# Split input weights kept in DRAM for the later token groups of a hybrid layer

## The chip, the cores and the metric

The kernel runs on one core of one Trainium2 chip. The metric is the device time of one execution in microseconds. Times of several executions are given by their median; one further execution was profiled, and all rows below come from it. Engines are called by the names of the profile: PE is TensorE (PEld its weight loads), DVE is VectorE, ACT is ScalarE, POOL is GpSimd, and SP is SyncE, whose queue here issues all DMAs.

## The reference

One layer, computed for two sets of streams that share the weights: one prompt of 2048 tokens without a past, and 8 running streams with 16 new tokens each. `D_MODEL` is 1024, the projection `w_in` has 7308 columns, all data is fp32.

```
def hybrid_layer(x, p, S_rwkv, shift, S_ssm, conv_buf, k_cache, v_cache):
    h = rms_norm(x, p['norm_w'])
    u = h @ p['w_in']
    ua, ga, zb, xbc, dtb, qc, kc, vc, gc = jnp.split(u, IN_SPLITS, axis=-1)
    oa, S_rwkv, shift = rwkv7_branch(ua, ga, S_rwkv, shift, p)
    ob, S_ssm, conv_buf = mamba2_branch(zb, xbc, dtb, S_ssm, conv_buf, p)
    oc, k_new, v_new = stick_breaking_branch(qc, kc, vc, gc, k_cache, v_cache, p)
    y = x + (jnp.concatenate([oa, ob, oc], axis=-1) @ p['w_out']).astype(x.dtype)
    return y, (S_rwkv, shift, S_ssm, conv_buf, k_new, v_new)
```

The RWKV-7 branch is a linear recurrence with a matrix state for each of 12 heads, the Mamba-2 branch a chunked scan with a convolution in front, the stick-breaking branch an attention whose weights come from a product of `1 - sigmoid` from the right. What the change touches is the second line, `h @ w_in`.

## The kernel before

**Groups.** The 2176 tokens are cut into four groups: 512 prompt tokens and all 128 tokens of the running streams in the first, 512 prompt tokens in each of the others. `h` of one group stays in SBUF, transposed, as a high part `hh` and a low part `hl`. The columns of `w_in` pass by once for every group, so each is loaded four times.

**Products in two parts.** PE multiplies in fp32r, which is fp32 rounded to fewer bits. So each factor is split: `whi` is the weight cast to fp32r on ACT, `wlo` is the rest, `raw - whi`, by a subtraction on POOL (helper `wsplit`, line 537). A product is three matmuls that add up in PSUM: `whi hh`, `whi hl` and `wlo hh`. Results go to PSUM tiles called `pd`.

**Weight tiles.** `wtile` (line 529) gives three tiles of 128 x 536: `wraw` from a ring of four, `whi` and `wlo` from rings of five each. Two functions load weights of the input:

- `wload(cols)` (line 542): 128 columns in two halves of 512 rows; a half is one DMA of 256 KB, one cast and one subtraction. It feeds `dense_t`, where the weights are stationary and up to 512 tokens stream. It is called 39 times in a group (RWKV's k, r, v, gate and low-rank columns, the convolution's channels, the attention's gate).
- `wload_n(spec)` (line 552): 256 columns (268 for one of them, which takes 12 columns of `dt` along by a second small DMA) in four quarters of 256 rows. It feeds `dense_n`, where 128 tokens are stationary and the columns stream. It is called 9 times in a group (q, k, v of the attention, the gate z of Mamba-2).

That is 39 x 2 + 9 x 4 = 114 pieces in a group and 456 in the program. The output projection of the first two branches, `project_ab` (line 590), takes tiles from the same rings for pieces of `w_out` and of the branch outputs `oT`; of those some are split on DVE, the others on POOL.

**Other names.** `fs` and `DN` (lines 989 to 999) are the small DVE operations by which RWKV inverts 16 x 16 blocks; they lie between a store of `GB` to the DRAM scratch `dA`, a load as `AT`, a store to `dD` and a load as `Da`. `RV`, `pz`, `py`, `SE`, `ZY` belong to RWKV's chain over chunks, `rq_m`, `rq_y` and `rq_t` to the inverse square roots, `ab` is a load of the scan's sums.

**What sets the order.** Instructions are not issued as the code is read. A planner (`class Plan`) collects a whole part of the program (the first group in two parts, then the other three groups in one, then the attention) and places instruction after instruction on its engine, always the one that can start first by a small cost model; rings of tiles are handed out in program order. The order that it finds is fixed for every engine and for the queue of SP. An instruction that waits holds up those behind it on its engine, and a DMA that waits for its slot holds up the DMAs behind it.

**Attention stage.** From 3048 us on no weights of the input are used any more.

Of the kernel before, what the change touches and what calls it, by code (L numbers as in the profile page):

```python
# [7 lines left out]
F32 = mybir.dt.float32  # L8
F32R = mybir.dt.float32r
# [423 lines left out]
def build(tc, nc, A, O):  # L433
    ctx = ExitStack()
    with ctx:
        _build(ctx, tc, nc, A, O)


def _build(ctx, tc, nc, A, O):
    plan = Plan(tc)  # L440
    V, S, G, T, Y = (plan.engine(e, x) for e, x in zip("VSGTY", (nc.vector, nc.scalar, nc.gpsimd, nc.tensor, nc.sync)))
# [4 lines left out]
    wp = ph.enter_context(tc.tile_pool(name="w", bufs=2))  # L446
# [6 lines left out]
    dr = ctx.enter_context(tc.tile_pool(name="scratch", bufs=1, space=DRAM))  # L453
# [4 lines left out]
    def pg():  # L458
        return pp.tile([128, 512], F32, name="pg", tag="pg", bufs=3)
# [10 lines left out]
    def f32(ap):  # L470
        return ap.bitcast(F32)
# [29 lines left out]
    win = A["w_in"][0]  # L501
# [24 lines left out]
        (eng_lo or V).tensor_tensor(lo, raw, f32(hi), ALU.subtract)  # L526


    def wtile(n):

        return [wp.tile([128, 536], F32 if nm == "wraw" else F32R, name=nm, tag=nm, bufs=4 if nm == "wraw" else 5)[:, 0:n]
                for nm in ("wraw", "whi", "wlo")]

    def tw(n):
        return wp.tile([128, 536], F32, name="tw", tag="tw", bufs=4)[:, 0:n]
# [1 line left out]
    def wsplit(raw, hi, lo, eng):  # L537
        S.copy(hi, raw)
        eng.tensor_tensor(lo, raw, f32(hi), ALU.subtract)
        return hi, lo  # L540

    def wload(cols):

        res = []
        for half in range(2):
            raw, hi, lo = wtile(512)
            Y.dma_start(raw.rearrange("p (k c) -> p k c", c=128),
                        win[512 * half:512 * half + 512, cols:cols + 128].rearrange("(k p) c -> p k c", p=128))
            res.append([x.rearrange("p (k c) -> p k c", c=128) for x in wsplit(raw, hi, lo, G)])
        return res  # L550

    def wload_n(spec):

        n = sum(c for _, c in spec)
        res = []
        for q in range(4):
            raw, hi, lo = wtile(2 * n)
            r3 = raw.rearrange("p (k c) -> p k c", c=n)
            o = 0
            for c0, cn in spec:  # L560
                Y.dma_start(r3[:, :, o:o + cn],
                            win[256 * q:256 * q + 256, c0:c0 + cn].rearrange("(k p) c -> p k c", p=128))
                o += cn
            res.append([x.rearrange("p (k c) -> p k c", c=n) for x in wsplit(raw, hi, lo, G)])
        return n, res

    def dense_t(h, w, c, n):
# [90 lines left out]
    def sb_weights(kind, j):  # L658

        c0 = {"q": C_Q, "k": C_SK, "v": C_SV}[kind]  # L660
        return wload_n([(c0 + 256 * j, 256)] + [(C_DT, 12)] * (kind == "q" and j == 0))
# [63 lines left out]
    def sb_gate(g, h, j):  # L725
        w = wload(C_SG + 128 * j)
        for u in g.pieces:
            p = dense_t(h, w, u.c0, u.n)
            o = tw(u.n)
            silu2(o[:, :u.n], p[:, :u.n], u.n)  # L730
            for c, n, t in g.segs(u.c0, u.n):
                Y.dma_start(gS[j, :, t:t + n], o[:, c - u.c0:c - u.c0 + n])
# [56 lines left out]
    def rwkv_pre(g, h, pool):  # L789
        w = wload(C_LO)  # L790
        ws, as_ = [x[:, 0:512] for x in h[2:4]] or [pool.tile([128, g.n], F32R, name=x, bufs=1) for x in ("ws", "as")]
        for u in g.pieces:
            n = u.n
            c = slice(u.c0, u.c0 + n)
            p = dense_t(h, w, u.c0, n)
            us = tw(n)
            shift(g, pool, p, u, 18, us)
            th = tw(n)[0:64]
            S.activation(th, us[0:64], AF.Tanh)
            V.tensor_copy(ws[0:64, c], th)  # L800
            V.tensor_tensor(ws[64:128, c], th, f32(ws[0:64, c]), ALU.subtract)
            V.tensor_copy(as_[64:128, c], us[64:128])
            V.tensor_tensor(as_[0:64, c], us[64:128], f32(as_[64:128, c]), ALU.subtract)
        return ws, as_

    def rwkv_dense(g, h, pr, pool, nms, D):
        for nm in nms:
            c0 = {"k": C_K, "r": C_R, "v": C_V, "g": C_G}[nm]
            w = wload(c0 + 128 * pr)
            if nm == "v":  # L810
                full = pool.tile([128, g.n + 128], F32, name="usv", tag="usv", bufs=2)
                G.memset(full[:, 0:64], 0.0)
                G.memset(full[:, 64 + g.n:128 + g.n], 0.0)
                D[nm] = full
                o = full[:, 64:64 + g.n]
            else:
                D[nm] = o = pool.tile([128, g.n], F32, name="us" + nm, tag="us" + nm, bufs=2 if nm == "k" else 1)
            for u in g.pieces:
                p = dense_t(h, w, u.c0, u.n)
                oc = o[:, u.c0:u.c0 + u.n]  # L820
                if nm == "g":
                    silu2(oc, p[:, :u.n], u.n)
                else:
                    shift(g, pool, p, u, c0 // 128 + pr, oc)
# [542 lines left out]
    def ssd_parts(g, h, pool, nb):  # L1367
# [25 lines left out]
        def gates(j):  # L1393

            w = wload_n([(C_Z + 256 * j, 256)])
            if j == 1:
                z1 = st["z"] = pool.tile([128, nt, 128], F32, name="zz", tag="zz", bufs=1)
            for ti, (c, p0) in enumerate(g.tiles):
                p = dense_n(h, w, c)
                z = tw(256)  # L1400
                if j == 1:
                    s = tw(256)
                    S.activation(s, p[:, 0:256], AF.Tanh, scale=0.5)
                    V.scalar_tensor_tensor(z[:, 0:128], s[:, 0:128], 1.0, p[:, 0:128], ALU.add, ALU.mult)
                    V.scalar_tensor_tensor(z1[:, ti, :], s[:, 128:256], 1.0, p[:, 128:256], ALU.add, ALU.mult)
                    gate(0, ti, 256, z[:, 0:128])
                else:
                    silu2(z, p[:, 0:256], 256)
                    gate(j // 2, ti, 64 * j, z)
                    if j == 2:  # L1410
                        gate(1, ti, 0, st["z"][:, ti, :])
# [130 lines left out]
    def following(gi, nh):  # L1542

        ng = GROUPS[gi + 1]
        rs = []
        return [lambda: rs.append(h_scale(ng.tiles))], [lambda: nh.extend(stage_h(ng, rs[0]))], pieces(ng, nh, "v0 q0 v1 k0 q1 k1")
# [47 lines left out]
    for i in range(2):  # L1594
        o = 64 * i
# [9 lines left out]
    for i in range(2):  # L1605
        o = 64 * i
# [41 lines left out]
    p = pg()  # L1648
# [54 lines left out]
    p = pg()  # L1703
# [7 lines left out]
    p = pg()  # L1711
# [12 lines left out]
    for d in dD:  # L1724
        m = NCH * 8 * 2064 + 128
        for i in range(0, m, 128 * 323):
            n = min(128 * 323, m - i)
# [14 lines left out]
    with tc.tile_pool(name="r0", bufs=1) as pool:  # L1742
        rw.send((pool, fill))
        w = tw(512).rearrange("p (a c) -> p a c", c=128)
        p = pg()
# [16 lines left out]
    with tc.tile_pool(name="r", bufs=1) as pool:  # L1762
        for gi in range(1, len(GROUPS)):
            g = GROUPS[gi]
            h, nh, fill = nh, [], {}
            gates = [lambda j=j, h=h: sb_gate(g, h, j) for j in range(4)]
            prj = [lambda a=a: project_ab(*a, lambda: wtile(512), pd, lambda: tw(512)) for a in proj_parts(GROUPS[gi - 1])]
            parts = ssd_parts(g, h, pool, 1)

            late, dense = prj[-1:], prj[:-1] + gates  # L1770
            a, b = parts[1:13], parts[13:]
            s = [parts[0]] + a[:5]
            for l in (a, b):
                if l is b:
                    s += b[:5]
                for f in l[5:9]:
                    s += [f] + dense[:1]
                    dense = dense[1:]
                s += l[9:]
            spread(fill, s + dense, 0, 10)  # L1780
            if gi + 1 < len(GROUPS):
                f8, f, x = following(gi, nh)
                fill[7].extend(f8)
                fill.setdefault(10, []).extend(f + late)
                fill.setdefault(11, []).extend(x)
            else:
                fill.setdefault(11, []).extend(late)
            st = stage_rwkv(g, h, pool, 3)
            next(st)
            st.send((pool, fill))  # L1790
        plan.emit()


    with tc.tile_pool(name="fin", bufs=1) as pool:
        r = pool.tile([64, 6, 128], F32, name="r")
        for q in range(2):
            p = pg()
# [7 lines left out]
        for q in range(2):  # L1805
            p = pg()
# [6 lines left out]
        p = pg()  # L1813
# [25 lines left out]
    p = pt()  # L1839
# [240 lines left out]
```

## Time and profile before

| | |
|---|---|
| runs | 3867.2 us median of 3 (3865.2 to 3870.8) |
| the profiled execution | 3871.6 us, its span 3869.9 us |
| instructions | 68238 |
| mean granted clock of PE | 0.933 |
| bytes moved | 454 MB, a mean of 117 GB/s |
| busy time of POOL and ACT on splits of weights and of `oT` (`wlo`, `whi`) | 762.4 us (568 subtractions), 428.7 us (702 casts) |

The span is the time from the first to the last instruction in the profile. A row of a group of instructions reads: line, engine, operation, out<-in by the program's names, shapes, count, then busy us and mean ns of one, then the engine's idle time in front of them and what ended it. All instructions are recorded at the one line where the planner issues them (L420), so groups are told apart by their tiles. A row of one tile reads: count, then shortest, median and longest ns. A row of waits reads: who waited for whom, us in total, times, longest us. The chain of work is followed back from the last instruction, at each step to what released it.

### The profile page before, as it was taken

Reading aid. Unit: us, or ns where it says so; the run is one execution under the profiler, and the core shown is the slowest. Engines: PE = TensorE matmul, PEld = TensorE weight load, DVE = VectorE, ACT = ScalarE, POOL = GpSimd, SP = SyncE. Lnnn points to the kernel's source line nnn. Section 1 sums busy time; section 2 is a strip of 40 time slices with the busy share of each in tenths; the row PEclk is TensorE's granted clock in tenths of the full one; section 3 lists DMA queues with packets and bytes.
Section 4 is the critical chain, followed back from the end, with each engine's and each line's share of the span. In section 5 each row is a group of like instructions: output and inputs, shape, how many; then the busy total and the mean of one; then the engine's idle time right before and its main releaser. Section 6 shows DMA issues by size and latency. Waiting matters only on the chain. (4 is left out here: it accounts for less than half of the span.)

```text
span 3869.9 us, 68238 instructions
## 1 busy us (share of the span) xinstructions
PE 3385.2 (87%) x23086; PEld 2749.6 (71%) x23086; DVE 2746.8 (71%) x6621; ACT 1724.5 (45%) x4134; POOL 1672.4 (43%) x2621
## 2 busy tenths in 40 slices
PE   7988999977988898988889998888999688989998
PEld 7877888867776676776667777766777555666665
DVE  7657778876698778657886875688778553456665
ACT  4544444433454444434444443445444343445554
POOL 4544555434555655644456555445555323000000
PEclk9998999978989899999899999989999889999999
DMA  4332333335425433553254336324532587765542
GB/s 120 97 107 61 95 92 78 78 103 145 121 59 158 140 89 101 153 149 94 71 154 110 78 84 180 101 68 128 150 82 64 154 212 223 176 150 140 135 129 66
DMA packets 693227, 454.41 MB, mean 117 GB/s; under 512 B 259978, under 2 KB 617806, under 8 KB 692878
## 3 DMA queue, kind: packets, MB, share of 16 engines
q1 hardware_dynamic: 692878, 450.06, 43.7%
q8 instruction: 183, 3.00, 0.3%
q14 instruction: 166, 1.36, 0.1%
HBM read 362.40 MB, written 87.51 MB: 116 GB/s over the span
## 5 line engine op out<-in xcount | busy, mean ns | idle before, releaser
L420 POOL TENSOR_TENSOR wlo<-wraw,whi 128x512 fp32r<-128x512 f32 (+1 forms) x568 | 762.4, 1348 | 542.0 <-ACT whi L420 378.9
L420 ACT CAST whi<-wraw 128x512 fp32r<-128x512 f32 (+1 forms) x702 | 428.7, 620 | 407.7 <-PE pd L420 290.7
L420 PE MATMUL pd<-hh,whi 128*128 128x512 f32 (+1 forms) x1560 | 552.8, 390 | 13.6 <-ACT tw L420 10.7
L420 PE MATMUL pd<-hh,wlo 128*128 128x512 f32 (+1 forms) x1560 | 553.2, 389 | 4.4 <-POOL wlo L420 4.4
L420 PE MATMUL pd<-hl,whi 128*128 128x512 f32 (+1 forms) x1560 | 555.9, 390 | 0.0
L420 PEld LDWEIGHTS pd<-hh,whi 128*128 128x128 f32 x1560 | 296.0, 196 | 51.3 <-ACT tw L420 14.3
L420 PEld LDWEIGHTS pd<-hh,wlo 128*128 128x128 f32 x1560 | 296.3, 194 | 39.5 <-POOL wlo L420 6.4
L420 POOL TENSOR_SCALAR SE<-RV,ELl 64x64 f32<-64x64 f32 x384 | 208.1, 542 | 267.7 <-DVE RV L420 218.8
L420 PEld LDWEIGHTS pd<-hl,whi 128*128 128x128 f32 x1560 | 296.8, 195 | 34.4 <-issue 1.5
L420 PE MATMUL pd<-whi,hh 128*128 128x256 f32 (+1 forms) x1224 | 300.1, 299 | 6.2 <-DVE tw L420 3.7
L420 PE MATMUL pd<-wlo,hh 128*128 128x256 f32 (+1 forms) x1224 | 298.4, 298 | 1.3 <-POOL wlo L420 1.3
L420 PE MATMUL pd<-whi,hl 128*128 128x256 f32 (+1 forms) x1224 | 295.5, 295 | 0.2 <-DVE hl L420 0.2
L420 DVE TENSOR_TENSOR_SCAN I<-ke,I,zeros 128x512 f32<-128x512 f32 x192 | 231.8, 1266 | 82.6 <-ACT ke L420 82.6
L420 ACT COPY aT<-pt 128x512 f32<-128x512 f32 (+3 forms) x320 | 162.4, 524 | 201.8 <-PE pt L420 199.2
L420 PEld LDWEIGHTS pd<-whi,hh 128*128 128x128 f32 x1224 | 214.8, 198 | 11.4 <-DVE tw L420 4.1
L420 PE MATMUL pt<-ident,I 128*128 128x128 f32 x1088 | 180.1, 286 | 42.2 <-DVE I L420 35.9
L420 PE MATMUL zt<-kk,qt 128*128 128x512 f32 (+3 forms) x640 | 205.8, 411 | 11.7 <-DMA kk<-kS 5.7
L420 PEld LDWEIGHTS pd<-wlo,hh 128*128 128x128 f32 x1224 | 213.8, 198 | 3.0 <-POOL wlo L420 2.0
L420 PEld LDWEIGHTS pd<-whi,hl 128*128 128x128 f32 x1224 | 213.0, 198 | 1.8 <-DVE hl L420 0.4
L420 POOL TENSOR_TENSOR oc<-oc,gy 128x512 f32<-128x512 f32 x16 | 20.8, 1302 | 438.2 <-ACT aT L420 167.1
L420 DVE TENSOR_TENSOR fs<-AT,DN 32x63 f32<-32x63 f32 (+14 forms) x672 | 199.6, 297 | 12.3 <-POOL DN L420 0.5
L420 PEld LDWEIGHTS pt<-ident,I 128*128 128x128 f32 x1088 | 120.4, 143 | 115.0 <-issue 36.9
(408 smaller groups left out, 8176.7 us busy)
## 6 DMA issues: line engine op xcount, KB each, us to landing
wraw<-in_w_in SPq DMA_DIRECT2D x456, 256.0 KB
wraw<-in_w_out SPq DMA_DIRECT2D x168, 256.0 KB
kk<-kS SPq DMA_DIRECT2D x160, 256.0 KB
wraw<-oT SPq DMA_DIRECT2D x78, 256.0 KB
ab<-acS SPq DMA_DIRECT2D x34, 384.0 KB
Da<-dD SPq DMA_DIRECT2D x96, 128.0 KB
sraw<-in_x_prompt SPq DMA_DIRECT2D x48, 256.0 KB
pr<-in_w_out SPq DMA_DIRECT2D x48, 256.0 KB
```

The source lines that it names most:

```text
L420: r = f(*a, **k).ins
```

## The change

The first group loads and splits a piece as before, and then stores both parts to a DRAM scratch tile of its own, `wS`, one for each set of columns. When another group asks for the same columns, a single DMA brings both parts back, and there is no raw load, no cast and no subtraction. For this `whi` and `wlo` become the two halves of one tile, `whl`, 128 x 2 x 536, from a ring of five; `wraw` keeps its ring of four. Pieces of `w_out` and `oT` in `project_ab` are still split in every group, with tiles of the same rings. A store is 512 KB, and so is a load of both parts.

```diff
+    def whl(n):
+        return wp.tile([128, 2, 536], F32R, name="whl", tag="whl", bufs=5)[:, :, 0:n]
+
+    def wraw(n):
+        return wp.tile([128, 536], F32, name="wraw", tag="wraw", bufs=4)[:, 0:n]
+
     def wtile(n):
-        return [wp.tile([128, 536], F32 if nm == "wraw" else F32R, name=nm, tag=nm, bufs=4 if nm == "wraw" else 5)[:, 0:n]
-                for nm in ("wraw", "whi", "wlo")]
+        x = whl(n)
+        return wraw(n), x[:, 0], x[:, 1]
+
+    wS = {}
+
+    def wparts(key, q, pieces, n, load):
+        x = whl(n)
+        if q not in wS.setdefault(key, []):
+            if not wS[key]:
+                wS[key].append(dr.tile([pieces, 128, 2, n], F32, name=f"wS{len(wS)}"))
+            wS[key].append(q)
+            raw = wraw(n)
+            load(raw)
+            wsplit(raw, x[:, 0], x[:, 1], G)
+            Y.dma_start(wS[key][0][q], f32(x))
+        else:
+            Y.dma_start(f32(x), wS[key][0][q])
+        return x[:, 0], x[:, 1]
...
     def wload(cols):
...
-            raw, hi, lo = wtile(512)
-            Y.dma_start(raw.rearrange("p (k c) -> p k c", c=128),
-                        win[512 * half:512 * half + 512, cols:cols + 128].rearrange("(k p) c -> p k c", p=128))
-            res.append([x.rearrange("p (k c) -> p k c", c=128) for x in wsplit(raw, hi, lo, G)])
+            def load(raw):
+                Y.dma_start(raw.rearrange("p (k c) -> p k c", c=128),
+                            win[512 * half:512 * half + 512, cols:cols + 128].rearrange("(k p) c -> p k c", p=128))
+            res.append([x.rearrange("p (k c) -> p k c", c=128) for x in wparts(cols, half, 2, 512, load)])
```

`wload_n` is changed in the same way, with `tuple(spec)` as the key and four pieces of `2 * n` columns.

More of the change, by code (lines that the diff above doesn't have):

```diff
@@ L556, in wload_n, with load @@
         for q in range(4):
[L557 to L564, printed above, removed]
+            def load(raw):
+                r3 = raw.rearrange("p (k c) -> p k c", c=n)
+                o = 0
+                for c0, cn in spec:
+                    Y.dma_start(r3[:, :, o:o + cn],
+                                win[256 * q:256 * q + 256, c0:c0 + cn].rearrange("(k p) c -> p k c", p=128))
+                    o += cn
+            res.append([x.rearrange("p (k c) -> p k c", c=n) for x in wparts(tuple(spec), q, 4, 2 * n, load)])
         return n, res
```

## The prediction

> **What bounds the kernel now.** I read the page first, then the busy time by stretches, then the chain of work, and last the weight tiles by themselves. The stretches are cut where the work changes: up to 930 us mostly the first group, up to 3048 us mostly groups two to four, behind that the attention stage.
>
> ```profile
> PE 3385.2 (87%) x23086; PEld 2749.6 (71%) x23086; DVE 2746.8 (71%) x6621; ACT 1724.5 (45%) x4134; POOL 1672.4 (43%) x2621
> 0.00:930.00 930.00, 812.73 (x6545) 734.67 (x6546) 683.19 (x2005) 401.53 (x1085) 455.66 (x945) 0.93 0.37 96
> 400.00:600.00 200.00, 185.81 (x1681) 167.86 (x1680) 158.19 (x502) 85.33 (x244) 108.05 (x251) 1.00 0.37 90
> 930.00:3048.00 2118.00, 1860.21 (x11874) 1525.92 (x11872) 1615.93 (x4105) 929.93 (x2236) 1129.59 (x1556) 0.93 0.41 112
> 3048.00:3870.00 822.00, 712.30 (x4669) 488.98 (x4669) 447.70 (x513) 393.05 (x814) 87.18 (x121) 0.94 0.60 156
> 2473.00:3010.00 537.00, 482.19 (x3131) 387.59 (x3132) 438.38 (x1153) 244.77 (x601) 294.20 (x427) 0.94 0.36 94
> ```
>
> Behind a stretch and its length stand the busy us of PE, PEld, DVE, ACT and POOL, then the granted clock, the DMA share and GB/s. In the later groups (930 to 3048) PE is busy 88% of the time and idle for 258 us; DVE is busy 76%, POOL 53%, ACT 44%. PE is the fullest, but the chain of work of the last whole group (2473 to 3010) says that it is not alone:
>
> ```profile
> by line: PE pd L420 23.1%; PE pg L420 9.1%; DVE DN L420 5.3%; DVE fs L420 5.0%; issue 4.7%; POOL wlo L420 4.7%; DVE BK L420 4.1%; DVE ST L420 4.1%; PE pz L420 3.6%; DVE tw L420 3.6%; ACT tw L420 1.9%; PE py L420 1.8%; DVE wlo L420 1.7%; DMA
> ```
>
> The names shown hold 72.7% of that stretch: PE 37.6, DVE 23.8, POOL 4.7, the rest ACT and issue. The path goes back and forth between PE and DVE, so what delays DVE delays the group. What delays DVE is in the timeline, a weight split on POOL beside the small DVE operations of the RWKV inverse:
>
> ```profile
> 1904.61 1.27 POOL L420 TENSOR_TENSOR wlo<-wraw,whi 128x512 fp32r<-128x512 f32 x1 [2.15 <-ACT whi L420]
> 1904.64 1.30 DVE L420 TENSOR_TENSOR fs<-AT,DN 32x55 f32<-32x55 f32 x1
> 1906.72 0.20 DVE L420 TENSOR_TENSOR fs<-AT,DN 32x48 f32<-32x48 f32 x1
> 1908.02 1.67 POOL L420 TENSOR_TENSOR wlo<-wraw,whi 128x512 fp32r<-128x512 f32 x1
> 1908.47 1.27 DVE L420 TENSOR_TENSOR fs<-AT,DN 32x39 f32<-32x39 f32 x1
> L420 DVE TENSOR_TENSOR fs<-AT,DN x504: 151/201/1342, 1027.0 to 2980.1; 32x28 f32<-32x28 f32 x24, 32x55 f32<-32x55 f32 x24, 32x39 f32<-32x39 f32 x24, 32x60 f32<-32x60 f32 x24
> L420 DVE TENSOR_TENSOR DN<-DN,fs x504: 152/200/1368, 1027.3 to 2980.4; 32x28 f32<-32x28 f32 x24, 32x55 f32<-32x55 f32 x24, 32x39 f32<-32x39 f32 x24, 32x60 f32<-32x60 f32 x24
> 930.00:3048.00 2118.00, 298.88 (x1008) 0.93 0.41 112
> ```
>
> The same kind of instruction takes 0.20 us alone and 1.30 us when a POOL `wlo` holds something that both need; both DVE instructions end with the POOL one. The last row, of the tile `fs` alone, is the mean: 298.88/1008 = 297 ns against a median of 200, so about 97 us are lost in these two lines alone. I did the same for every DVE instruction from 930 to 3048: its duration less the 15th percentile of its own kind and shape, counted where that is over 0.1 us and a POOL `wlo` overlaps it most. That gives 276 instructions with 275 us lost; the first and the last of them, each with its POOL partner:
>
> ```profile
> 936.45 1.28 POOL L420 TENSOR_TENSOR wlo<-wraw,whi 128x512 fp32r<-128x512 f32 x1 [1.18 <-ACT whi L420]
> 936.61 1.15 DVE L420 TENSOR_SCALAR rq_m<-sss 128x8 f32<-128x8 f32 x1
> ...
> 3046.63 2.97 POOL L420 TENSOR_TENSOR wlo<-wraw,whi 128x512 fp32r<-128x512 f32 x2 [0.27 <-ACT whi L420]
> 3047.15 1.23 DVE L420 TENSOR_TENSOR rq_t<-rq_y 128x4 f32<-128x4 f32 x1
> ```
>
> **The change part by part.** The weights of the input are 456 pieces, 114 in each of four groups.
>
> ```profile
> L420 POOL TENSOR_TENSOR wlo<-wraw,whi 128x512 fp32r<-128x512 f32 (+1 forms) x568 | 762.4, 1348 | 542.0 <-ACT whi L420 378.9
> L420 ACT CAST whi<-wraw 128x512 fp32r<-128x512 f32 (+1 forms) x702 | 428.7, 620 | 407.7 <-PE pd L420 290.7
> wraw<-in_w_in SPq DMA_DIRECT2D x456, 256.0 KB
> 930.00:3048.00 2118.00, 104.55 (x134) 345.25 (x567) 583.76 (x432) 0.93 0.41 112
> L420 SPq DMA_DIRECT2D wraw<-in_w_in x472: 367/374/1724, 7.8 to 2976.8; - x158
> ```
>
> *Removed: 342 splits.* In groups two to four 342 casts (0.620 us) leave ACT, 212 us, and 342 subtractions (1.348 us) leave POOL, 461 us. Neither engine is full, so as busy time this is worth nothing; it counts through DVE. The fourth row is the tile `wraw` alone: 432 POOL subtractions from 930 on, which cost DVE 275 us, 0.64 us each. So 342 x 0.64 = 217 us of DVE time go. How much of it lies on the path: at least the named DVE rows, 23.8% of 537 = 128 us of 438 busy, a share of 0.29; at most all that is not named otherwise as well (23.8 + 27.3 = 51.1%, 274 us), 0.63. I split the unnamed part as the named one, 23.8/72.7 = 0.33 of the path, 176 us of 438, a share of 0.40. That is -87 us (bounds -63 and -137). What is late next is PE: its best 200 us show it 93% busy, and 1860/0.93 = 2000 would be 118 us less than the 2118, so PE leaves room for 87 but not for 137.
>
> The Trainium skill, "SBUF — State Buffer", section "Who interferes with whom", says of this row that a VectorE instruction with two SBUF inputs and a GpSimd instruction that reads SBUF exclude each other, and that the one that comes second is blocked for the first one's whole length. The trace agrees, 1.30 against 0.20 us. Taken alone the rule would let each subtraction block DVE for all of its 1.35 us, 461 us in all; the measured 0.64 us says that DVE meets about half of it.
>
> *Removed from the path itself: POOL `wlo`.* It has 4.7% of the chain shown; by 342/432 of that over 2118 us this would be -79 us. But the wait for a weight does not vanish, the landing of a DMA takes its place, so I take 0 for both together and keep -79 as an end.
>
> *Changed: 342 loads.* They now bring 512 KB straight into the five slots of the parts, where a 256 KB load went into one of four raw slots ahead of them.
>
> ```profile
> 2657.97 2.57 DMA ab<-acS
> 2670.75 2.54 DMA wraw<-in_w_out
> GB/s 56 0 0 0 0 0 0 0 0 0 0 0 0 256 323 348 364 338 343 353 287 10 0 0 0 0 0 82 0 0 0 0 0 0 0 0 0 0 0 0
> 1909.61 0.39 PE L420 MATMUL pd<-hh,whi 128*128 128x512 f32 x1
> 1909.84 0.39 PE L420 MATMUL pd<-hh,wlo 128*128 128x512 f32 x1
> ACT whi L420 <- PE pd L420: 214.8, 164, 7.1
> PEld pd L420 <- POOL wlo L420: 21.9, 35, 3.0
> PE pd L420 <- POOL wlo L420: 11.0, 19, 2.6
> SPq L420 <- POOL wlo L420: 620.5, 254, 11.7
> ```
>
> From the end of a slot's last matmul to its next use there were a cast and a subtraction, 0.62 + 1.35 = 2.0 us and what their engines were busy with. Now there is an issue of 0.37 us and a landing: 2.5 us for 256 KB, and another 256 KB at about 340 GB/s (the third row, where one load runs alone) is 0.8 us, so 3.7 us, 1.7 us more. The cover is the ring: matmuls of 512 columns start 0.23 us apart, a piece has 12 of them, 2.8 us, and with one piece in use four others lie ahead, 11 us. So I cost it at nothing; today's waits of PE on the split, 21.9 + 11.0 = 33 us, stand for what becomes a wait on the DMA. Without the cover it is 342 x 1.7 = 581 us, the outer bound on the slow side. The bytes: 342 x 256 KB more over 2118 us are 42 GB/s on top of 112, which by the share per GB/s lifts 0.41 to 0.56; the attention stage lives with 0.60.
>
> SP now waits for PE's last read where it waited for POOL 254 times, 620 us in all. Behind such a wait stand `ab`, the round trip of the RWKV inverse through `dA` and `dD`, stores and loads of other tiles. One blocking wait replaces another of about the same number, so 0, bounds -20 to +40 us (a 254th part of 620, 2.4 us, on every third of some 50 such DMAs of the chain, to either side).
>
> *Added: 114 stores of 512 KB in the first group.* SP issues 114 x 0.37 = 42 us more, each behind the subtraction it waits for; 60 MB over 930 us are 64 GB/s, which lifts its share from 0.37 to 0.61. The split stays there, so DVE gains nothing. A slot is held until the store has read it, while PE reads the same slot for 2.8 us after the split, which hides most of it. I take +5 us, bounds 0 and +42.
>
> *Untouched:* the attention stage, 822 us. The planner makes a new order with its own costs; I take +0, give or take 10.
>
> **Sum.** -87 + 0 + 0 + 0 + 5 = -82 us. The profiled execution took 3871.6 us (span 3869.9), so 3789.6; it lies 4.4 us above the median of 3867.2, so the median comes to 3785 us, 2.1% less.
>
> **The rivals.** First, *off the path*: DVE gives its 217 us back as idle time, because the dense matmuls of PE, 23.1% of the chain, close every gap. For it: PE 88% busy. Against it: 258 us of idle PE, and DVE rows with a quarter of the chain. Time 3867.
>
> Second, *both ends pay*: the upper DVE share and the `wlo` of the chain go too. -137 - 79 is more than PE leaves at its present clock, but the clock of 0.93 would rise with fewer gaps (1.00 in the row 400 to 600). PE's room of 118 plus half of the 7% of 2118 us, 74, is -192, with +5: 3680. For it: ACT and POOL get free besides. Against it: PE would have to be as dense all through as in its best stretch.
>
> Third, on the other side, *late weights*: with nine pieces under way before (five split, four raw) and five now, PE waits for landings of the parts, in `PEld pd`, released by a DMA. For it: in 164 casts of 567 the slot had just been freed by PE, so the ring is already short at times, and projection pieces, with six matmuls, use a slot in 1.4 us. Against it: PE waited for the split only 33 us. It turns the result when the 342 loads cost more than 82/342 = 0.24 us each; at half of the 1.7 us, +291 - 82, it is 4076; at 0.4 us, 3922.
>
> Fourth, *the stores hold the ring*: the slots of the first group come free only when a store has landed, 2.5 us by the row above, 290 us if all of it shows; it decides from 0.72 us a store. Then 3785 + 100 = 3885 for a third. Against it is PE's own use of the slot. The Trainium skill, "DMA: Bandwidth & Descriptors", section "Anatomy of one DMA", puts most of a fixed cost of about 2 us down to the receipt of the write and calls HBM the heaviest target. By that figure it would be, as an estimate, 114 x 2.0 = 228 us; no run shown here has a store from this ring.
>
> That the later groups would not find their parts can be left out: the page's 456 pieces are four times 114, the same columns.
>
> **How the numbers follow.** Forecast 0.70 (3730 to 3850), off the path 0.08, both ends pay 0.08, late weights 0.10, stores 0.04. Within 0.2%, 8 us, is about what a measurement of this kernel can tell from no change. Faster: 0.70 + 0.08 and a little of the first rival, 0.80; same 0.07; slower 0.13. The range, with the lower bounds of the unknown costs and up to where the gain is nearly gone: 3700 to 3862; beneath it lies half of the second case, above it the slow ones and most of the first.
>
> **What would show it.** In the later groups POOL loses about 461 us and ACT 212; the mean of `fs` and `DN` falls from 297 towards 225 ns; DVE's busy time from 930 on falls by about 200 us; PE's share there rises from 88 to 91 or 92%. Wrong would be: DVE falls as said and PE's share does not rise (off the path); large waits of `PEld pd` on `DMA whl<-wS` (late weights); a first group that is longer by over 20 us (stores).

## The result and the profile after

The changed kernel takes 3691.6 us (median of 4 runs, 3687.4 to 3698.0) against 3866.2 us before: a ratio of 0.9555, with a 95% interval of 0.9535 to 0.9574. That is 175 us less, where 82 were forecast, and 3691.6 us lies under the range of 3700 to 3862. The head of the changed kernel's page, its bytes, and the shares of its chain by engine:

```profile
span 3688.1 us, 67232 instructions
PE 3306.9 (90%) x23086; PEld 2683.9 (73%) x23086; DVE 2524.9 (68%) x6621; ACT 1530.7 (42%) x3792; POOL 1210.8 (33%) x2279
HBM read 452.20 MB, written 147.37 MB: 163 GB/s over the span
PE 50%; DVE 28%; issue 6%; ACT 6%; DMA 6%; POOL 3%; SPq 1%; DVEq 0%; POOLq 0%; ACTq 0%
```

POOL has lost 461.6 us, the 342 subtractions, and ACT 193.8, where 212 were forecast for the casts. DVE has as many instructions as before (6621) and yet is busy for 222 us less, close to the 217 us forecast. PE has the same 23086 matmuls and is busy for 78 us less. Its mean granted clock was 0.956 against 0.933 before, and busy time times clock is nearly the same (3161 and 3158 us), so the higher clock accounts for the 78 us.

Next the stretches of the changed kernel, cut at the same places of the work: groups two to four end at 2875 us now. The row with one pair of numbers is of the tile `fs` alone (DVE), and the last two are rows of the whole chain between 2310 and 2830 us, and of the tiles `fs` and `DN`.

```profile
930.00:2875.00 1945.00, 1802.66 (x12021) 1481.10 (x12020) 1406.10 (x4128) 754.32 (x1923) 696.87 (x1240) 0.97 0.56 169
2875.00:3688.00 813.00, 702.43 (x4669) 481.65 (x4669) 446.10 (x512) 392.96 (x814) 88.14 (x120) 0.96 0.61 157
930.00:2875.00 1945.00, 226.47 (x1008) 0.97 0.56 169
by line: PE pd L420 38.3%; PE pg L420 9.1%; issue 4.9%; DVE ST L420 3.7%; DVE DN L420 3.1%; DVE BK L420 3.0%; DVE fs L420 2.5%; DMA whl<-wS 2.5%; PE pz L420 2.4%; DVE tw L420 1.9%; PE py L420 1.8%; DVE RV L420 1.7%; DVE whl L420 1.5%; DVE Y
```

PE's share of the later groups went from 88 to 93%, its idle time from 258 to 142 us, its clock from 0.93 to 0.97. `fs` and `DN` fell from 297 to 225 ns a piece (226.47/1008). On the chain PE's dense matmuls, `PE pd`, have 38% of this stretch of the last group, where they had 23% of the prediction's (the two stretches do not begin at quite the same place of the work).

The first copy `ZY<-pz` of each group's RWKV chain is a good marker of the same point of the work. Differences between markers give each part its own time (the last column is taken before rounding):

| from the first `ZY` of a group to that of the next | before | after | difference |
|---|---|---|---|
| head, up to the first group's | 376 | 391 | +14 |
| first group | 641 | 648 | +7 |
| second | 754 | 688 | -66 |
| third | 727 | 645 | -82 |
| fourth (to the last `ZY`) | 542 | 494 | -47 |
| rest, with the attention | 831 | 823 | -9 |

So the head and the first group pay 21 us, and the later ones bring 195.

What PE and SP wait for in the changed kernel, 930 to 2875 us:

```profile
PEld pd L420 <- DMA whl<-wS: 13.2, 18, 2.1
PE pd L420 <- DMA whl<-wS: 13.0, 16, 1.9
SPq L420 <- PE pd L420: 410.4, 192, 9.9
```

The loads of both parts make PE wait for 26 us in all. SP now waits for PE, 192 times, where it waited for POOL 254 times.

### The profile page after: what moved, and what is told of

Same layout as the page of the kernel before. It is cut to its first block, busy times and chain, and to the rows that moved or that the text cites. A ratio compares the mean times of both kernels' runs of the same rounds, so it can differ in the third digit from the quotient of the medians.

```text
span 3688.1 us, 67232 instructions
## 1 busy us (share of the span) xinstructions
PE 3306.9 (90%) x23086; PEld 2683.9 (73%) x23086; DVE 2524.9 (68%) x6621; ACT 1530.7 (42%) x3792; POOL 1210.8 (33%) x2279
## 4 chain that ended last, share of the span: by engine, by line
PE 50%; DVE 28%; issue 6%; ACT 6%; DMA 6%; POOL 3%; SPq 1%; DVEq 0%; POOLq 0%; ACTq 0%
PE pd L420 28%; PE pg L420 7%; DVE I L420 5%; PE ot L420 3%; PE acc L420 3%; PE pz L420 3%; PE pt L420 3%; DVE tw L420 2%; PE py L420 2%; DVE ST L420 2%; DVE DN L420 2%; DMA whl<-wS 2%; DVE rq_t L420 2%; DVE BK L420 2%; PE zt L420 2%
## 5 line engine op out<-in xcount | busy, mean ns | idle before, releaser
L420 PE MATMUL pd<-hh,whl 128*128 128x512 f32 (+1 forms) x3120 | 957.2, 385 | 12.8 <-ACT tw L420 4.3
L420 PEld LDWEIGHTS pd<-hh,whl 128*128 128x128 f32 x3120 | 563.8, 193 | 81.4 <-ACT tw L420 7.1
L420 PE MATMUL pd<-hl,whl 128*128 128x512 f32 (+1 forms) x1560 | 543.9, 384 | 0.0
L420 PE MATMUL pd<-whl,hh 128*128 128x256 f32 (+1 forms) x2448 | 482.4, 294 | 22.7 <-DMA whl<-wS 8.9
L420 PEld LDWEIGHTS pd<-whl,hh 128*128 128x128 f32 x2448 | 377.6, 194 | 35.7 <-DMA whl<-wS 12.7
L420 POOL TENSOR_TENSOR whl<-wraw,whl 128x512 fp32r<-128x512 f32 (+1 forms) x226 | 304.9, 1354 | 242.2 <-ACT whl L420 205.6
L420 PE MATMUL pd<-whl 128*128 128x512 f32 x936 | 298.1, 436 | 21.8 <-POOL whl L420 10.7
L420 PEld LDWEIGHTS pd<-hl,whl 128*128 128x128 f32 x1560 | 291.7, 193 | 31.2
L420 ACT CAST whl<-wraw 128x512 fp32r<-128x512 f32 (+1 forms) x360 | 220.4, 620 | 198.9 <-PE pd L420 110.7
L420 PE MATMUL pd<-whl,hl 128*128 128x256 f32 (+1 forms) x1224 | 302.9, 293 | 0.0
L420 PE MATMUL zt<-kk,qt 128*128 128x512 f32 (+3 forms) x640 | 203.0, 407 | 10.9 <-DMA kk<-kS 4.8
```

Of the source, the lines that this page charges most:

```text
L420: r = f(*a, **k).ins
```

## The experiments

Two things were open: whether DVE's blocked time makes the gain, or the freed queues of POOL and ACT, or a new order of the planner; and why it is twice the forecast.

**One order, four runs.** To keep the order of the work fixed, the planner of the changed kernel was shown a cast and a subtraction after each load of both parts, and when it had placed everything, each was either issued or not. Their result has no reader.

```diff
             Y.dma_start(f32(x), wS[key][0][q])
+            raw = wraw(n)
+            plan.alt = nothing                     # or None: issue it
+            S.copy(raw, f32(x[:, 0]))
+            plan.alt = nothing                     # or None, or sets
+            G.tensor_tensor(raw, f32(x[:, 0]), f32(x[:, 1]), ALU.subtract)
+            plan.alt = None
```

Neither issued (the ghost run):

> The changed kernel, but the planner is shown a cast on ACT and a subtraction on POOL after each load of both parts (on the loaded parts, into a raw tile that nobody reads); neither is issued. So this is the order of the work that goes with these operations, without them. Theory A (DVE was blocked by the subtractions, and nearly all of what it lost lay on the path): within 20 us of the changed kernel, 3675 to 3715. Theory C (the planner's new order made most of the gain): at least 60 us slower than the changed kernel, 3750 or more. Theory B (POOL's and ACT's queues held up other work): as A.

Measured 3685.3 us (3681.4 to 3696.1), 6 us below the changed kernel, and the two spreads overlap. So none of the gain comes from the order that the planner finds when these operations are not in its plan.

The subtraction issued:

> The same planned order, and the subtraction is issued on POOL (342 of 1.35 us, reading both parts, the result goes nowhere); PE does not wait for it. Theory A: DVE loses some 217 us again and the time goes up by 150 to 220 us, to 3840 to 3910. Theory B (what counted was that weights waited for the split): no wait of PE on it, so at most 40 us above the run without it.

Measured 3885.0 us (3878.6 to 3894.1), 200 us more than without. The subtraction has no reader, so PE waits for no split here. A slot of the parts is held until POOL has read it, but that costs little: from 800 to 3040 us PE and its weight loads wait 39 us for the loads of the parts, against 31 us with neither issued. Their waits for `GB`, a result of DVE, rise from 23 to 90 us.

Memsets in its place:

```diff
+    def sets(o, *a, **k):
+        return [nc.gpsimd.tensor_copy(o[:, 0:1], a[0][:, 0:1]), nc.gpsimd.memset(o[:, 0:512], 0.0),
+                nc.gpsimd.memset(o[:, 0:512], 0.0), nc.gpsimd.memset(o[:, 0:256], 0.0)]
```

> The same planned order, and in the place of each subtraction POOL has a copy of one column and three memsets of 512, 512 and 256 columns into the same raw tile, about as long together (1.4 us) but without reading. Theory A: POOL is as busy but DVE is not blocked: within 40 us of the run with nothing issued. Theory B (POOL's queue is busy and holds up SE, ysb and others): as slow as the run with the subtraction.

Measured 3710.2 us (3694.9 to 3719.1), 25 us more than with nothing, though its own runs spread over 24 us. The stretches of the later groups in the three runs (nothing, subtraction, memsets), each with its row of the tile `fs` behind it:

```profile
930.00:2875.00 1945.00, 1805.63 (x12057) 1486.65 (x12056) 1415.93 (x4139) 756.03 (x1926) 706.36 (x1241) 0.97 0.56 169
930.00:2875.00 1945.00, 222.41 (x1008) 0.97 0.56 169
```

```profile
930.00:3058.00 2128.00, 1875.11 (x12061) 1537.34 (x12060) 1614.13 (x4140) 756.25 (x1926) 1143.95 (x1570) 0.94 0.51 155
930.00:3058.00 2128.00, 295.77 (x1008) 0.94 0.51 155
```

```profile
930.00:2896.00 1966.00, 1820.48 (x12066) 1498.67 (x12065) 1421.50 (x4138) 755.54 (x1926) 1219.47 (x2563) 0.96 0.55 167
930.00:2896.00 1966.00, 224.60 (x1008) 0.96 0.55 167
```

POOL is at least as busy with the memsets (1219 us) as with the subtraction (1144), but the subtraction lengthens DVE by 198 us with one instruction more, and the memsets by 6. Only with the subtraction do `fs` and `DN` go back to 293 ns; beside the memsets they take 223, with nothing 221. So it is hardly that POOL is busy; it is that both read SBUF. This is the rule of the Trainium skill, "SBUF — State Buffer", section "Who interferes with whom", and the trace agrees with its second half too: a GpSimd instruction that only writes does not contend with VectorE's second input.

Both issued:

> The same planned order, with the cast on ACT (342 of 0.62 us) and the subtraction on POOL issued, both without a reader. Theory A: at most 25 us above the run with the subtraction alone, because ACT has room. Theory B: ACT's casts stand in front of the copies of RWKV's chain: 50 us or more above it.

Measured 3883.0 us (3879.2 to 3884.0): the cast's 342 x 0.62 us on ACT cost nothing that can be seen. This kernel has all the engine work of the kernel before and ends 18 us behind it (3864.8 in the same comparison). That would be the stores, less what the loads bring; the two were not measured apart here.

**Is it DVE's time, or its being blocked?** Each blocked us cost almost one us of time. The next two runs put work of DVE's own there instead, 342 subtractions of 0.68 us, once in the plan and once unknown to the planner, in the place of POOL's.

```diff
+            V.tensor_tensor(wraw(n), f32(x[:, 0]), f32(x[:, 1]), ALU.subtract)          # planned
...
+    def unplanned(o, *a, **k):
+        return nc.vector.tensor_tensor(o[:, 0:512], nwb[:, 0:512], nwb[:, 512:1024], ALU.subtract)
```

> The changed kernel, and behind each load of both parts a subtraction of the two on DVE into a raw tile that nobody reads: 342 of 0.68 us, 233 us of DVE time that the planner knows of. Theory A (DVE's time is on the path whatever it does): 190 to 235 us slower, 3880 to 3925. Rival (blocking costs so much because the order was made without it, and work that is in the plan is put into DVE's idle time): at most 120 us slower, below 3812.

> The order of the ghost run (cast and subtraction in the plan, neither issued), with a subtraction of 512 columns issued on DVE in the place where the planner put POOL's: the same 342 of 0.68 us as in the run with planned DVE work, on tiles that are always ready, but the planner does not know that DVE is busy there. Theory D (what costs is DVE time that the order does not allow for, whether by blocking or by work): 170 to 235 us above the ghost run, 3855 to 3920. Theory E (blocking is worse than work of DVE's own, planned or not): as with planned work, 40 to 90 us above the ghost run, 3725 to 3775.

Measured 3753.6 us (3744.8 to 3755.7) with planned work and 3778.5 us (3776.2 to 3787.8) with unplanned work: 62 us above the changed kernel and 93 above the ghost run. Their rows of the added instruction, planned and unplanned:

```profile
L420 DVE TENSOR_TENSOR wraw<-whl x342: 653/683/1579, 817.9 to 2890.8; 128x512 f32<-128x512 f32 x165, 128x536 f32<-128x536 f32 x6
```

```profile
L549 DVE TENSOR_TENSOR wraw<-nwb x342: 655/683/1565, 822.6 to 2923.2; 128x512 f32<-128x512 f32 x171
```

At 342 x 0.683 = 234 us of added work that is 0.27 and 0.40 us of time for each us, against 200/198 = 1.0 for DVE's blocked time. By DVE's busy time over the whole span the comparison comes out alike: planned work adds 200 us to it, unplanned work 205, blocking 207. The expectation that any delay which the order does not allow for costs nearly its full length did not hold: unplanned work cost 93 us, far under the 170 to 235 of that theory and just above the 40 to 90 of the other. So blocking is dearer than as much work.

**The split on DVE.** If blocking is what costs, the subtraction can be moved instead of saved. In the kernel before, without any parts in DRAM:

```diff
-            res.append([x.rearrange("p (k c) -> p k c", c=128) for x in wsplit(raw, hi, lo, G)])
+            res.append([x.rearrange("p (k c) -> p k c", c=128) for x in wsplit(raw, hi, lo, V)])
```

(and the same in `wload_n`)

> The kernel before, with the subtraction of all 456 input pieces on DVE (0.68 us each, 311 us) and none of them on POOL, where they cost DVE about 375 us of blocked time over the whole program (100 us beside them up to 1130 us, 275 us from 930 on). Theory A (DVE time is what counts): DVE's own time falls by some 65 us and the time by 30 to 70 us, to 3795 to 3835. Rival (work on DVE that the planner knows of is placed where it does no harm, blocking is not): below 3790. Rival (DVE's own work is worse than being blocked): above 3865.

Measured 3637.4 us (3633.0 to 3642.1), a ratio to before of 0.9406 (0.9381 to 0.9431): faster than the change. The band worked out from DVE's sum of time missed, and the first rival, by which planned work finds DVE's gaps and blocking does not, was right. (The expectation's two stretches overlap from 930 to 1130 us, so about 23 of its 375 us are counted twice.) DVE's busy time fell by only 28 us, from 2746.8 to 2719.2, and the kernel's time by 229.

Then the same in the changed kernel for the first group, which still splits, and for the output projection's pieces as well:

```diff
-            wsplit(raw, x[:, 0], x[:, 1], G)
+            wsplit(raw, x[:, 0], x[:, 1], V)
...
-                wsplit(raw, wh, wl, V if k // kw % every == 0 else G)
+                wsplit(raw, wh, wl, V)
```

> The changed kernel with the first group's 114 subtractions on DVE instead of POOL. They block DVE for 71 us in the first 1130 us of the changed kernel. Theory A with the price of planned work (0.27 us a piece's us, 114 x 0.68 x 0.27 = 21 us, against 71 x 0.95 = 67): 40 to 55 us faster than the changed kernel, 3636 to 3652. Rival (the first group is bound by its stores now): within 15 us of the changed kernel.

> As the run before, and the pieces of the output projection are all split on DVE too (128 more subtractions from POOL to DVE, 112 of them before the attention stage). They block DVE for 74 us from 1130 us on. By the same prices 74 x 0.95 = 70 saved and 112 x 0.68 x 0.27 = 21 spent: 3590 to 3610. Rival (DVE becomes full): no gain on the run before.

> The kernel before with every subtraction of weights on DVE, those of the output projection as well; no parts in DRAM. By the same prices 40 to 55 us faster than with the input weights alone on DVE, 3582 to 3600. Rival (DVE at 75% there has no more room): 3625 or more.

Measured 3640.0 us (3638.3 to 3650.1), 3592.0 us (3586.9 to 3592.7) and 3588.9 us (3585.9 to 3594.1); all three inside their bands, with the prices of the runs above. The second moved 136 subtractions of the output projection, not 128 (POOL has 2165 instructions in the first and 2029 in the second). The last two, with and without parts in DRAM, are equal: the best kernel here is the kernel before with its splits moved to DVE, a ratio of 0.9287 (0.9269 to 0.9304). Its engines, behind those of the changed kernel with all splits on DVE:

```profile
PE 3286.3 (92%) x23086; PEld 2678.5 (75%) x23086; DVE 2529.2 (70%) x6871; ACT 1530.7 (43%) x3792; POOL 909.0 (25%) x2029
```

```profile
PE 3300.8 (92%) x23086; PEld 2683.2 (75%) x23086; DVE 2727.6 (76%) x7213; ACT 1721.4 (48%) x4134; POOL 945.1 (26%) x2029
```

Without the parts DVE works 198 us and ACT 191 us longer and the time is the same. By the markers the parts cost 41 us up to the second group (984 against 943 us) and bring 35 from there to the last `ZY` (1790 against 1826).

**The stores alone.**

```diff
+        raw = wraw(n)
+        load(raw)
+        wsplit(raw, x[:, 0], x[:, 1], G)
         if q not in wS.setdefault(key, []):
...
             Y.dma_start(wS[key][0][q], f32(x))
-        else:
-            Y.dma_start(f32(x), wS[key][0][q])
```

> The first group stores its parts as in the changed kernel, and the later groups load and split the raw weights as before, so the stores are there and nothing is gained from them. Theory A (the stores cost the first group some 20 us, as the markers of its end stand 22 us later in the changed kernel): 3880 to 3892 against 3865. Rival: the first group is longer only because the planner orders it otherwise with one ring for both parts: also 3880 or more, but then with no more waits on stores or on DMAs than before. Forecast of record: +5, 3870.

Measured 3917.1 us (3915.1 to 3926.1), a ratio of 1.0134 (1.011 to 1.0157): 50 us, more than either account said. The markers put +18 into the head, +18 into the first group and +15 into the later ones. Up to 400 us there is one wait of PE on a DMA of over 2 us, where the kernel before has none, and the changed kernel has the same, with the same row:

```profile
PE pg L420 <- DMA Da<-dD: 10.9, 1, 10.9
```

The load of the inverse's result comes late once, and PE stands for 10.9 us. In the changed kernel SP has just waited 14.3 us for a DVE result, and then three stores of parts and three raw loads stand in its queue between the stores to `dD` (the last at 354.5 us) and the load `Da` (359.8 us); in the kernel before, `Da` follows 1.8 us behind them. The other 25 us up to the second group are not tied to a wait. The run also has the new order and one ring for both parts, so neither these 25 us nor the 15 us of the later groups are shown to be the stores' own.

**The ring.**

```diff
-        return wp.tile([128, 2, 536], F32R, name="whl", tag="whl", bufs=5)[:, :, 0:n]
+        return wp.tile([128, 2, 536], F32R, name="whl", tag="whl", bufs=4)[:, :, 0:n]
```

> The changed kernel with a ring of four tiles for the parts instead of five. Theory A (the ring covers the landing of the parts): at most 25 us slower, 3690 to 3716. Rival (the loads are just in time, and the ring of five is already short): over 60 us slower, 3750 or more, with waits of PE on the landing of the parts.

Measured 3734.5 us (3724.2 to 3737.7), 43 us above the changed kernel, between the two accounts. PE's waits on the loads (930 to 2920 us) grow from 26 to 81 us:

```profile
PEld pd L420 <- DMA whl<-wS: 31.4, 24, 10.1
PE pd L420 <- DMA whl<-wS: 49.8, 34, 9.6
```

So five slots nearly hide the landing here and four do not: the cover is one slot thick.

## Why the prediction was half right

*The mechanism* was right and shown: the gain comes from DVE's time blocked beside POOL's subtraction. The subtraction put back brought 200 us back; a POOL that is busy without reading brought at most 25, the cast on ACT and the planner's order nothing.

*The amount of blocked time* was right: 217 us forecast, DVE's busy time fell by 222, and by 198 between the two runs of one order.

*The share of it on the path* was the step that failed. It was put at 0.40, the chain's share of all of DVE's time, which made -87 us of 217 blocked. It measured about 1.0 with POOL's 25 us in it (200 us of time for 198 blocked) and 0.9 without; in the changed kernel the later groups gained 195 us. Ordinary DVE work at the same places did cost 0.40 (unplanned) and 0.27 (planned), so 0.40 was a fair price for work, but not for blocking. Two things in the traces go towards the difference; neither was tried alone. First, the blocked instructions are not a fair sample of DVE's time. Followed one by one through the chain of the kernel before, from 2473 to 3010 us, 45 of the 67 us blocked beside `wlo` lie on the chain (47 of 66 instructions), 0.67 where all of DVE's time has 0.44; in the run with the subtraction put back it is 123 of 168 us, 0.73, over 1278 us. A likely reason, not tested, is that an instruction is blocked only when DVE has come to it, whereas added work can fall into DVE's idle time. The prediction used the average although the trace it had allowed the count. Second, PE's clock: with the same matmuls PE is busy for 1806 us at a clock of 0.97 without the subtraction and for 1875 us at 0.94 with it. Only the subtraction differs between these two runs, so the clock rose because of it; that fewer gaps raise the clock fits, but is not shown (in the run with the input weights' splits on DVE, PE was busy 91% of the span at a clock of 0.948, in the changed kernel 90% at 0.956). The prediction had the clock in a rival, *both ends pay*, at 3680 us with a chance of 0.08, and near that the time came out. Its mechanism was half right: more of DVE's time lay on the path and the clock rose, but the `wlo` of the chain as a supplier of PE was not needed, so that it hit the time is in part luck. How the 200 us divide between the two was not measured apart.

*PE's room.* "PE leaves room for 118 us" took PE's best stretch as a bound at a fixed busy time. PE reached that 93% over all later groups, and its busy time there fell by 58 us too, so that stretch became 173 us shorter.

*The loads* at 0 were right: PE waits 26 us for them where it had waited 33 for the split. The cover of 11 us, four slots ahead against an issue and a landing of 3.7 us, was too kind, since one slot less cost 43 us.

*SP's other waits* at 0 fit, but were not tried alone.

*The stores* at +5 were too small, though inside the bounds of 0 and +42: the changed kernel is 21 us longer up to the second group, where the prediction had named over 20 us as the sign of the stores, the run with the stores alone 36, and 41 lie between the two kernels with all splits on DVE. All three have the one ring and the new order with the stores. The sum had priced SP's issues and the holding of a slot; the one load that PE is seen to wait for is of another tile, behind the stores in SP's queue. The figure of 2.0 us that the fourth rival takes from the Trainium skill, "DMA: Bandwidth & Descriptors", section "Anatomy of one DMA", stands there for DMAs issued by GpSimd; the stores here are issued by SP.

*Untouched:* what follows the last `ZY`, with the attention stage, came out 9 us shorter, inside the 10.

Of the other rivals, *off the path* and *late weights* are ruled out by the runs; *stores hold the ring* has its direction right and a size of 21 to 41 us instead of a hundred.

## What to carry to other kernels

Look in the timeline for DVE instructions that end together with a POOL instruction and are far longer than their kind's median: that is blocked time, and here each us of it cost 0.9 to 1.0 us of the kernel, two to four times as much as work of DVE's own. Count such time instruction by instruction on the chain instead of taking the engine's share of it. A subtraction of two SBUF tiles that takes 1.35 us on POOL and 0.68 on DVE may well be better on DVE even where DVE is the fuller engine, if whoever orders the work knows of it: moving all of them brought 7%, and saving the work by way of DRAM added nothing to that.

## What the runs showed of the hardware that was not expected

A one-input DVE instruction on 8 columns was held for 1.15 us beside a POOL subtraction too (the row of `rq_m` in the prediction; the median of its kind is 0.17 us), not only those with two inputs. Memsets on POOL, which only write, left the two-input `fs` and `DN` alone (223 ns against 293 beside the subtraction), but not every one-input instruction: `rq_y<-rq_m` took 0.55 us where its median is 0.18, beside the first of the two memsets of the second row, which alone took 0.53 us and ended 0.02 us before it.

```profile
974.43 0.55 DVE L421 TENSOR_SCALAR rq_y<-rq_m 128x8 int32<-128x8 int32 x1
974.42 0.90 POOL L551 MEMSET wraw<- 128x512 f32 x2
```

Counted as in the prediction, 53 DVE instructions lost 15 us beside the memsets from 930 to 2896 us, most of them with one input. PE's granted clock over the later groups was 0.97 without POOL's subtractions and 0.94 with them, with nothing else changed, and the same 12,060 matmuls took 69 us less busy time without.
